# A two-layer streaming encoder on one core: the set-up gets its squares from a token-major copy of the input

## The chip, the cores and the metric

The kernel runs on one core of a Trainium2 chip. The metric is the device time of one execution in microseconds (us). Three runs of the kernel before took 1355.7, 1358.24 and 1358.74 us; the median is 1358.24 us.

The engines are named as in the profile: PE (TensorE, matrix multiplies; PEld is its weight loading), DVE (VectorE), ACT (ScalarE), POOL (GpSimd), SP (SyncE, whose queue issues the DMAs here). Each engine takes its own instructions in the order in which they stand in its queue: an instruction that waits holds everything behind it.

## The reference

512 tokens of width 1024 go through two layers, each a token mixer and a squared-ReLU MLP with residual additions, and a last RMSNorm. All is float32. What matters here is the beginning of the first mixer:

```python
y = _rmsnorm(h, norm_mix[0])            # h * rsqrt(mean(h*h) + eps) * w
proj = y @ w_in                         # 1024 -> 4112 columns
qkv  = silu(causal_conv(proj[..., :3072]))   # 8 heads of q, k, v
a, b = proj[..., 4096:4104], proj[..., 4104:]
beta = sigmoid(b)
g    = -exp(a_log) * softplus(a + dt_bias)   # log decay of each head
q, k = l2norm(q), l2norm(k)
o    = gated_delta_rule(q, k, v, beta, g)    # chunked, with a triangular solve per head
```

After it come the gate, the output projection, an MLP, the second layer (HGRN2 and an MLP), and the final norm.

## The kernel before

The input is kept with channels on the 128 partitions: eight tiles x[c] of 128 channels by 512 tokens. A product with a weight matrix is made exact enough by splitting both sides in two parts of a shorter float type: weights into `whi` and `wlo` (a cast by ACT, line 114, a subtraction by DVE or POOL, line 115), activations into `yh` and `yl` (lines 216 to 219). For each of the eight channel tiles k, a block of 128 output columns takes three matmuls: whi with yh, whi with yl, wlo with yh (lines 125 to 127). A block is thus 24 matmuls of 128x128 by 512 into one PSUM bank, called `pj`. Weights come in pairs of blocks: a raw tile of 128x8x256 (1 MB), split into whi and wlo.

The RMSNorm's factor (one number per token) is not needed for the products: they are made of x*w, and the factor, `rB`, multiplies the result when DVE takes it out of PSUM (line 389, tile `z`). So the sum of squares may come late.

`setup` loads x and the first two weight pairs in slices of 1, 1, 2, 2 and 2 channel tiles, so that the first four blocks can start early. For each x[c], ACT makes yh and squares x (lines 160, 163), DVE makes yl, and POOL or DVE adds the square to `sqacc` (line 165). For pair 0 POOL makes wlo, for pair 1 DVE. Two matmuls on a tile of zeros (line 240, `warm`) run before the first data is there.

`gdn` then asks for six blocks (four of the wide first group and two of the third pair), and after them issues, at high priority, `rstd_rows` and `gdn_decay`: `rstd_rows` splits sqacc, sums it over partitions with two matmuls into `ps` (line 195), and computes rB on rows of 512 (lines 197 to 206, ACT with Ln and Exp between). `gdn_decay` multiplies all of y by the 16 columns for a and b: 16 matmuls of 32 columns into `pab` (line 335); from pab*rB follow the cumulated log decays through `pt`, `pg` and `prow` (lines 337 to 378).

Then head by head: `gdn_conv` takes three blocks out of PSUM (line 389) and applies the four-tap convolution (a scale by ACT, line 391, three multiply-adds by DVE, line 393) into `kq` (k and q of a head side by side) and `v`; `gdn_silu` applies SiLU on ACT (line 85), with a table load before and after (line 91); `gdn_local` transposes k, q and v on PE (`pk` line 436, `pq` 443, `pv` 456), and makes the decay mask (`pe`, `e`, line 465) and the chunk products (`pga` line 475, `n`, `aa`). After every second head `gdn_inverse` solves two heads' triangular systems with many 32x32 matmuls (`px`, `pu`).

The order on each engine is not the program's order: the framework schedules the whole program before the run, by modelled times and priorities, and the result is fixed: whatever is late on the chip, each engine keeps the listed order. Tiles come from pools with a fixed number of buffers per name; a new tile waits until an old one of that name is free. In the trace SP issues a DMA, once eight are under way, when the one eight before it has landed.

Of the kernel before, what the change touches and what calls it, by code (L numbers as in the profile page):

```python
# [23 lines left out]
EPS = 1e-6  # L24
WARM = 384
# [8 lines left out]
class Net:  # L34
# [62 lines left out]
    def weight_tiles(self):  # L97
# [4 lines left out]
        return (tile("raw", F32, 2), *(tile(t + "3", F32R, 1) if last else tile(t, F32R, 2) for t in ("whi", "wlo")))  # L102
# [64 lines left out]
    def rstd(self):  # L167

        nc = self.nc
        ps = self.mix("ps")  # L170
        for c in range(NC):
            nc.tensor.matmul(ps[:, c:c + 1], lhsT=self.sq[:, c * P:(c + 1) * P], rhs=self.ones,
                             start=True, stop=True)
# [49 lines left out]
    def renew(self, c, norm, sq_eng="g", act=False):  # L223

        with self.tc.high_priority(offset=3000 if c == NB - 1 else 0):
            self.y[c] = self.split_norm(c, self.nw[:, norm * NB + c:norm * NB + c + 1], act)
            self.square_into(c == 0, self.h[c], sq_eng)


    def setup(self, w):  # L230

        nc = self.nc
# [3 lines left out]
        zeros = self.work("gate", bufs=2)  # L236
        nc.vector.memset(zeros, 0.0)
        warm = self.mix("warm", [P, WARM])
        for _ in range(2):
            nc.tensor.matmul(warm, lhsT=zeros[:, 0:P], rhs=zeros[:, 0:WARM], start=True, stop=True)  # L240
# [21 lines left out]
        return [(hi, lo) for _, hi, lo in pairs]  # L262
# [8 lines left out]
    def gdn(self, first):  # L271
        nc, a = self.nc, self.a
# [9 lines left out]
        abraw = self.work("gate", [P, NB, 2 * NH], bufs=2)  # L282
        nc.sync.dma_start(out=abraw, in_=a["gdn_ab"])
        ab = self.work("x", [P, NB, 4 * NH], F32R)
        hi = ab[:, :, 0:2 * NH]
        nc.scalar.copy(out=hi, in_=abraw)
        nc.vector.tensor_tensor(out=ab[:, :, 2 * NH:], in0=abraw, in1=hi.bitcast(F32), op=ALU.subtract)
# [41 lines left out]
    def gdn_decay(self, ab, alog, dtb):  # L329

        nc = self.nc
        pab = self.mix("pab", [4 * NH, T])
        for k in range(NB):
            for i, y in enumerate(self.y[k]):
                nc.tensor.matmul(pab, lhsT=ab[:, k], rhs=y, start=(k == 0 and i == 0), stop=(k == NB - 1 and i == 1))
# [656 lines left out]
def layout(x, gdn_w_in, gdn_conv, gdn_a_log, gdn_dt_bias, gdn_onorm, gdn_w_out, hgrn_w_in, hgrn_lb_logits,  # L992
           hgrn_gnorm, hgrn_w_out, norm_mix, norm_mlp, mlp_w_up, mlp_w_down, norm_final):
    i = np.arange(P)
    block = lambda start, h: np.arange(start + h * P, start + (h + 1) * P)
    o = {"x": x[0].T.reshape(NB, P, T).transpose(1, 0, 2)}
# [40 lines left out]
```

## Time and profile before

| | |
|---|---|
| median of three runs | 1358.24 us |
| the profiled execution | 1358.3 us, of which the span of instructions 1356.4 us |
| PE busy | 1330.5 us (98%) |
| DVE / ACT / POOL busy | 820.1 / 547.0 / 170.8 us |
| granted TensorE clock, mean of the span | 0.994 |

The span runs from the first instruction to the last; 1.9 us lie outside it. [...] A view of waits names the engine and the instruction that an engine last waited for; a view of windows gives the busy time of every engine in a stretch, and the granted clock.

### The profile page before, as it was taken

What the parts mean: (1) busy time and instruction counts of PE and PEld (TensorE: products, weight loads), DVE (VectorE), ACT (ScalarE), POOL (GpSimd) and SP (SyncE); (2) the same over time, 40 slices, a digit from 0 to 9 for tenths busy, and PEclk for the clock granted to TensorE, in tenths of its full rate; (3) what the DMA queues carried; (4) which work ended last, traced back from release to release, by engine and by line L of the source; (5) the groups of instructions that cost most, each with busy time, mean ns of one, the idle gap of its engine ahead of it and who ended that gap; (6) DMA issues with size and microseconds to landing.
All of it is one profiled execution on the core that took longest, in us unless ns stands there. A gap on an engine that the chain in (4) does not pass through costs nothing.

```text
span 1356.4 us, 24202 instructions
## 1 busy us (share of the span) xinstructions
PE 1330.5 (98%) x10340; PEld 1102.9 (81%) x10340; DVE 820.1 (60%) x1408; ACT 547.0 (40%) x1016; POOL 170.8 (13%) x172
## 2 busy tenths in 40 slices
PE   7999999999999999999999999999999999999997
PEld 5777777877888888888888898898888888888897
DVE  5896877765944444444473897787674444445453
ACT  5663556454344214233123555545344313214242
POOL 4001020200200120201220010000100020110222
PEclk8999999999999999999999999999999999999999
DMA  6131111221332222222231311121142223232242
GB/s 200 40 118 35 62 64 34 79 79 64 124 113 100 94 97 93 94 93 94 93 97 42 111 65 64 64 94 64 63 155 93 93 96 113 93 104 93 93 141 78
DMA packets 23356, 121.57 MB, mean 90 GB/s; under 512 B 3664, under 2 KB 6864, under 8 KB 9680
## 3 DMA queue, kind: packets, MB, share of 16 engines
q1 hardware_dynamic: 23248, 120.02, 26.3%
q8 instruction: 81, 1.33, 0.4%
q14 instruction: 27, 0.22, 0.0%
HBM read 117.91 MB, written 2.10 MB: 88 GB/s over the span
## 4 chain that ended last, share of the span: by engine, by line
PE 89%; DVE 5%; ACT 2%; issue 1%; DMA 1%; POOL 0%; SPq 0%; POOLq 0%; DVEq 0%; ACTq 0%
PE pj L126 25%; PE pj L127 25%; PE pj L125 25%; PE pj L714 1%; PE pj L715 1%; PE pj L713 1%; PE pga L475 1%; PE gr L786 1%; PE pu L520 1%; PE px L513 1%; DVE whi L742 1%; DVE wlo L115 1%; PE pw L590 1%; DVE kq L393 1%; DVE ol L742 1%
## 5 line engine op out<-in xcount | busy, mean ns | idle before, releaser
L114 ACT CAST whi<-raw 128x1024 fp32r<-128x1024 f32 (+2 forms) x222 | 220.9, 1024 | 410.0 <-PE pj L126 396.6
L125 PE MATMUL pj<-yh,whi 128*128 128x512 f32 x960 | 381.0, 397 | 0.9 <-ACT whi L114 0.9
L126 PE MATMUL pj<-yl,whi 128*128 128x512 f32 x960 | 381.3, 397 | 0.0
L115 DVE TENSOR_TENSOR wlo<-raw,whi 128x1024 fp32r<-128x1024 f32 (+2 forms) x217 | 289.7, 1348 | 151.0 <-ACT whi L114 148.7
L127 PE MATMUL pj<-yh,wlo 128*128 128x512 f32 x960 | 380.0, 396 | 0.0
L125 PEld LDWEIGHTS pj<-yh,whi 128*128 128x128 f32 x960 | 181.7, 189 | 37.6 <-ACT whi L114 2.0
L126 PEld LDWEIGHTS pj<-yl,whi 128*128 128x128 f32 x960 | 181.9, 189 | 36.0
L127 PEld LDWEIGHTS pj<-yh,wlo 128*128 128x128 f32 x960 | 181.2, 189 | 36.2 <-POOL wlo L115 0.3
L126 PE MATMUL pj<-ol,whi 128*128 128x512 f32 x336 | 131.3, 391 | 0.0
L898 DVE TENSOR_TENSOR gate<-pj,rB 128x512 f32<-128x512 f32 x56 | 38.6, 691 | 148.2 <-PE pj L127 148.2
L125 PE MATMUL pj<-oh,whi 128*128 128x512 f32 x320 | 125.1, 391 | 0.0
L127 PE MATMUL pj<-oh,wlo 128*128 128x512 f32 x320 | 125.0, 391 | 0.0
L884 ACT ACTIVATE z<-pj 128x512 f32<-128x512 f32 x64 | 38.0, 594 | 113.7 <-PE pj L127 109.6
L900 POOL TENSOR_TENSOR kd<-kd,gate 128x512 f32<-128x512 f32 x18 | 23.3, 1293 | 462.2 <-DVE gate L898 462.2
L126 PEld LDWEIGHTS pj<-ol,whi 128*128 128x128 f32 x336 | 63.2, 188 | 13.0
L125 PEld LDWEIGHTS pj<-oh,whi 128*128 128x128 f32 x320 | 60.1, 188 | 12.5 <-issue 0.3
L127 PEld LDWEIGHTS pj<-oh,wlo 128*128 128x128 f32 x320 | 60.0, 188 | 12.2
L165 POOL TENSOR_TENSOR sqacc<-sqacc,z 128x512 f32<-128x512 f32 x25 | 38.0, 1519 | 245.9 <-ACT z L163 241.8
L127 PE MATMUL pj<-kq,wlo 128*128 128x512 f32 (+1 forms) x192 | 67.8, 355 | 0.5 <-DVE wlo L115 0.5
L125 PE MATMUL pj<-kq,whi 128*128 128x512 f32 (+1 forms) x192 | 68.0, 354 | 0.0
L126 PE MATMUL pj<-kq,whi 128*128 128x512 f32 (+1 forms) x192 | 67.9, 354 | 0.0
L742 DVE TENSOR_TENSOR whi<-whi 128x256 f32<-128x256 f32 x112 | 49.9, 447 | 6.4 <-ACT whi L745 4.8
(379 smaller groups left out, 1941.0 us busy)
## 6 DMA issues: line engine op xcount, KB each, us to landing
raw<-down SPq DMA_DIRECT2D x36, 1024.0 KB, 4.9
raw<-up SPq DMA_DIRECT2D x32, 1024.0 KB, 4.8
raw<-gdn_in SPq DMA_DIRECT2D x14, 1024.0 KB, 4.8
raw<-hgrn_fq SPq DMA_DIRECT2D x8, 1024.0 KB, 4.9
raw<-gdn_out SPq DMA_DIRECT2D x4, 1024.0 KB, 5.4
raw<-hgrn_i SPq DMA_DIRECT2D x4, 1024.0 KB, 5.0
raw<-hgrn_gate SPq DMA_DIRECT2D x4, 1024.0 KB, 4.8
raw<-hgrn_out SPq DMA_DIRECT2D x4, 1024.0 KB, 4.9
```

The costliest lines, as they stand in the source:

```text
L114: self.nc.scalar.copy(out=hi[:, k], in_=raw[:, k])
L115: eng.tensor_tensor(out=lo[:, k], in0=raw[:, k], in1=hi[:, k].bitcast(F32), op=ALU.subtract)
L125: mm(o, lhsT=hi[:, k, c], rhs=yh, start=(k == 0), stop=False)
L126: mm(o, lhsT=hi[:, k, c], rhs=yl, start=False, stop=False)
L127: mm(o, lhsT=lo[:, k, c], rhs=yh, start=False, stop=(k == NB - 1))
L165: e.tensor_tensor(out=self.sq, in0=self.sq, in1=t, op=ALU.add)
L393: nc.vector.scalar_tensor_tensor(out=dst[:, s:], in0=z[:, :T - s], scalar=w[:, 3 - s:4 - s], in1=dst[:, s:], op0=ALU.mult, op1=ALU.add)
L475: mm(pga[:, c - c2], lhsT=ck(k, c), rhs=kq[:, :, c * P:(c + 1) * P], start=True, stop=True)
L742: mul = lambda o, x, y: nc.vector.tensor_tensor(out=o, in0=x, in1=y, op=ALU.mult)
L884: nc.scalar.activation(out=z, in_=out, func=AF.Relu)
L898: nc.vector.tensor_tensor(out=t, in0=out, in1=self.r2b, op=ALU.mult)
L900: e.tensor_tensor(out=self.h[c], in0=self.h[c], in1=t, op=ALU.add)
```

## The change

1. The squares no longer come from the channel-major x. A second copy of the input, `xt`, four tiles of 128 tokens by 1024 channels (512 KB each), is loaded during the set-up, and ACT squares each with a sum over its row: `sums[:, c]` has the sum of squares of 128 tokens. The eight squares of x[c], the additions into sqacc and `rstd_rows` go for this first norm; `rstd(self.sums)` takes the sums, works on 128x4 numbers, and spreads the result by four small matmuls into `pb`, from which ACT copies rB.
2. All wlo of the set-up are made by DVE; POOL makes none.
3. The weights for a and b are loaded and split early (after the second slice). The 16 products into `pab` are issued in the program after the first four blocks and before the blocks of the third pair.
4. The third pair is loaded in `setup` in four quarters into free `ol` tiles, and split there; it takes no raw buffer. `stream` takes it from `first`.
5. `warm` is nine matmuls of 128x128 by 128 in place of two of 128x128 by 384, on a smaller zero tile.

```diff
-WARM = 384
+WARM = 9
...
+        first = first or [self.weights(src[i]) for i in range(wide)]
         if wide:
-            first = first or [self.weights(src[i]) for i in range(wide)]
-            yield from self.project([(w, b) for w in first for b in (0, 1)], y, tokens)
+            yield from self.project([(w, b) for w in first[0:wide] for b in (0, 1)], y, tokens)
         for i in range(wide, n):
-            w = self.weights(src[i])
+            w = first[i] if i < len(first) else self.weights(src[i])
...
-    def rstd(self):
+    def rstd(self, sums=None):
...
+        if sums is None:
+            sums = self.mix("ps")
...
-        nc.vector.tensor_scalar(out=x, in0=ps[:, 0:NC], scalar1=1.0 / D, scalar2=EPS,
+        nc.vector.tensor_scalar(out=x, in0=sums[:, 0:NC], scalar1=1.0 / D, scalar2=EPS,
...
+        self.sums = self.cp.tile([P, NC], F32, tag="sums", name="sums")
         start = 0
-        for end in (1, 2, 4, 6, 8):
+        for end, chunks in ((1, ()), (2, ()), (4, (0,)), (6, (1, 2)), (8, (3,))):
...
-                self.renew(c, 0, "g" if c % 2 or c == 0 else "v", act=True)
+                self.y[c] = self.split_norm(c, self.nw[:, c:c + 1], act=True)
             for i, (raw, hi, lo) in enumerate(pairs):
                 nc.sync.dma_start(out=raw[:, k], in_=w[i][:, k])
-                self.split_weights(raw, hi, lo, k, (nc.gpsimd, nc.vector)[i])
+                self.split_weights(raw, hi, lo, k, nc.vector)
+            for c in chunks:
+                t = self.work("kq", [P, 2 * T], bufs=4)
+                nc.sync.dma_start(out=t, in_=self.a["xt"][:, c])
+                nc.scalar.activation(out=t, in_=t, func=AF.Square, accum_out=self.sums[:, c:c + 1])
+            if end == 2:
+                raw = self.work("gate", [P, NB, 2 * NH], bufs=2)
+                nc.sync.dma_start(out=raw, in_=self.a["gdn_ab"])
...
         self.ident = self.const("ident", [P, P])
+        third = self.weight_tiles(raw=False)
+        for i in range(0, NB, 2):
+            raw = self.work("ol", [P, 2, 256], bufs=NH)
+            nc.sync.dma_start(out=raw, in_=w[2][:, i:i + 2])
+            self.split_weights(raw, *(t[:, i:i + 2] for t in third), slice(0, 2), nc.vector)
...
-        blocks = chain([next(blocks) for _ in range(6)], blocks)
+        ready = [next(blocks) for _ in range(4)]
+        pab = self.mix("pab", [4 * NH, T])
...
+                nc.tensor.matmul(pab, lhsT=self.ab[:, k], rhs=y, start=(k == 0 and i == 0),
+                                 stop=(k == NB - 1 and i == 1))
+        ready += [next(blocks) for _ in (0, 1)]
+        blocks = chain(ready, blocks)
         with self.tc.high_priority(offset=3000):
-            self.rb = self.rstd_rows()
-            self.gdn_decay(ab, alog, dtb)
+            self.rb = self.rstd(self.sums)[1]
+            self.gdn_decay(pab, alog, dtb)
```

The schedule of the first mixer comes out another way on every engine; from the output projection on, the engines' orders are the same as before.

On PE, among the first four blocks (pj_223 to pj_226), at the fifth channel tile (yh_146), the kernel before has:

```order
L126 MATMUL pj_223<-yl_147,whi_84 128x512
L127 MATMUL pj_223<-yh_146,wlo_85 128x512
L195 MATMUL ps_385<-z_381,one 128x512
L125 MATMUL pj_224<-yh_146,whi_84 128x512
L126 MATMUL pj_224<-yl_147,whi_84 128x512
L195 MATMUL ps_385<-z_382,one 128x512
L127 MATMUL pj_224<-yh_146,wlo_85 128x512
```

The two matmuls into ps, which need the finished sum of squares, stand before the last 45 of the 96 matmuls of the four blocks; 16 of pab follow 19 matmuls later.

In the changed kernel the four blocks are pj_238 to pj_241, and the first matmuls that need the squares (pb) stand at their very end, with the rest of pab behind:

```order
L126 MATMUL pj_241<-yh_181,whi_93 128x512
L127 MATMUL pj_241<-yl_182,whi_93 128x512
L183 MATMUL pb_415<-ident,rsr_409 128x128 x4
L128 MATMUL pj_241<-yh_181,wlo_94 128x512
L309 MATMUL pab_338<-yl_102,x_125 32x512
L309 MATMUL pab_338<-yh_113,x_125 32x512
```

So pab, which stood after 70 of the 96 matmuls of these blocks, now stands after all of them (but for one of its 16), and the squares are wanted 44 block matmuls later.

On PE before the transposes of the second head (pk_705, of kq_490), the kernel before has, after the last block of the third pair (pj_356):

```order
L127 MATMUL pj_632<-yh_131,wlo_595 128x512
L125 MATMUL pj_632<-yh_146,whi_594 128x512
L126 MATMUL pj_632<-yl_147,whi_594 128x512
L125 MATMUL pj_671<-yh_93,whi_664 128x512
L126 MATMUL pj_671<-yl_94,whi_664 128x512
L436 MATMUL pk_705<-ident,kq_490 128x128 x4
L443 MATMUL pq_718<-ident,kq_490 128x128 x4
L127 MATMUL pj_601<-yh_146,wlo_595 128x512
```

Between the end of pj_356 and pk_705 it has 30 matmuls of the next three blocks (14 of pj_601, 14 of pj_632, 2 of pj_671).

The changed kernel has at the same place, from the third matmul after the end of pj_380 (its last block of the third pair) to the transposes of the second head (pk_713, of kq_498):

```order
L126 MATMUL pj_640<-yh_101,whi_601 128x512
L473 MATMUL pv_561<-ident,v_475 128x128 x4
L479 MATMUL pe_570<-sqacc_467,both 128x512
L127 MATMUL pj_640<-yl_102,whi_601 128x512
L126 MATMUL pj_679<-yh_101,whi_671 128x512
L127 MATMUL pj_679<-yl_102,whi_671 128x512
L492 MATMUL pga_581<-kq_474 128x256 x2
L492 MATMUL pga_587<-kq_474 128x256 x2
L453 MATMUL pk_713<-ident,kq_498 128x128 x4
L460 MATMUL pq_726<-ident,kq_498 128x128 x4
L128 MATMUL pj_609<-yh_101,wlo_602 128x512
```

Six matmuls of the next three blocks stand there in place of 30; the other 24 have moved behind the second head's transposes.

On DVE the changed kernel has, up to the last multiply-add of kq_498:

```order
L494 SCALAR_TENSOR_TENSOR n_579<-pga_587,nd_546,e_521 128x128 x2
L496 TENSOR_TENSOR aa_580<-pga_587,e_521 128x256
L523 STREAM_TRANSPOSE xd_971<-n_579 32x128 x4
L410 SCALAR_TENSOR_TENSOR kq_498<-z_506,conv,kq_498 128x509
L410 SCALAR_TENSOR_TENSOR v_499<-z_512,conv,v_499 128x511
L116 TENSOR_TENSOR wlo_602<-raw_603,whi_601 128x1024
```

The work of the first head and the second head's convolution come in the same sequence as before, but the two splits of weights by DVE that stood among them (the third pair's second half and the fourth pair's first half) stand earlier and later.

## Rows read from the trace of the kernel before

**Rows 1.** The page: busy time of each engine, and the granted clock in 40 slices of 34 us.

```profile
PE 1330.5 (98%) x10340; PEld 1102.9 (81%) x10340; DVE 820.1 (60%) x1408; ACT 547.0 (40%) x1016; POOL 170.8 (13%) x172
...
PEclk8999999999999999999999999999999999999999
```

**Rows 2.** PE's waits from 0 to 130 us: what waited and for what, us in total, times, longest.

```profile
PE ps L195 <- ACT one L257: 5.3, 1, 5.3
PE pu L520 <- issue: 2.1, 1, 2.1
...
PE pk L436 <- ACT kq L85: 0.4, 1, 0.4
PE pv L456 <- ACT v L85: 0.4, 1, 0.4
PE px L553 <- DVE wlo L548: 0.3, 1, 0.3
```

**Rows 3.** The chain that ended last, from 17 to 26 us: start, length, what.

```profile
18.13 0.68 DVE wlo L115
18.81 1.20 DVE yl L219
...
20.41 0.74 DVE yl L219
21.15 0.61 DVE sqacc L165
...
21.90 1.66 POOL sqacc L165
...
23.59 0.62 ACT z L191
24.35 0.80 PE ps L195
```

**Rows 4.** Windows around that wait: stretch, length, busy us (and instructions) of PE, PEld, DVE, ACT, POOL, granted clock, DMA share, GB/s.

```profile
18.99:24.35 5.36, 0.02 (x2) 0.00 (x1) 3.56 (x6) 1.68 (x4) 3.40 (x3) 0.82 0.07 14
24.35:29.20 4.85, 4.85 (x11) 3.79 (x12) 2.30 (x3) 1.54 (x4) 1.52 (x3) 0.50 0.69 240
29.20:35.40 6.20, 6.20 (x28) 3.82 (x27) 2.69 (x5) 2.00 (x2) 0.00 (x0) 0.99 0.40 155
```

**Rows 5.** The timeline of ACT and PE in the first 13 us, in four places: start, length, engine, line, what. The rows are the first block matmuls, the first cast for the third channel tile, and the first and a later matmul at a shorter length.

```profile
5.25 1.22 PE L125 MATMUL pj<-yh,whi 128*128 128x512 f32 x2 [0.88 <-ACT whi L114]
...
8.82 0.40 PE L126 MATMUL pj<-yl,whi 128*128 128x512 f32 x1
...
10.95 0.60 ACT L114 CAST whi<-raw 128x512 fp32r<-128x512 f32 x1
...
12.51 0.39 PE L125 MATMUL pj<-yh,whi 128*128 128x512 f32 x1
```

**Rows 6.** The timeline of SP's queue: the issue of DMA 20, 24 and 27 (each when DMA 12, 16 and 19, of 256 KB, has landed).

```profile
12.37 0.33 SPq L58 DMA_DIRECT2D ident<-ident  x1
...
15.08 0.33 SPq L58 DMA_DIRECT2D ident<-ident  x1
...
17.08 0.33 SPq L58 DMA_DIRECT2D onorm<-onorm  x1
```

**Rows 7.** The chain that ended last, near 722 us: the four spreading matmuls of a later norm in the same form as the new ones.

```profile
722.50 0.97 PE pb L180 x8
```

**Rows 8.** PE's timeline at half and at full clock, and up to the transposes of the second head.

```profile
26.65 0.63 PE L125 MATMUL pj<-yh,whi 128*128 128x512 f32 x1
...
27.07 0.63 PE L126 MATMUL pj<-yl,whi 128*128 128x512 f32 x1
...
64.05 0.39 PE L125 MATMUL pj<-yh,whi 128*128 128x512 f32 x1
64.27 0.39 PE L126 MATMUL pj<-yl,whi 128*128 128x512 f32 x1
...
64.96 0.60 PE L436 MATMUL pk<-ident,kq 128*128 128x128 f32 x4
```

**Rows 9.** One window, from the start of DVE's pab*rB to the end of the second head's last multiply-add into kq; then DVE's group of weight splits in that window (count, busy us, mean ns of one).

```profile
35.44:63.68 28.24, 28.15 (x136) 22.71 (x135) 25.38 (x68) 19.36 (x46) 1.61 (x2) 1.00 0.11 38
...
L115 DVE TENSOR_TENSOR wlo<-raw,whi 128x1024 fp32r<-128x1024 f32 x2 | 2.4, 1209 | 0.0
```

**Rows 10.** ACT's timeline: the SiLU of the second head's kq, with its wait.

```profile
63.78 1.06 ACT L85 ACTIVATE kq<-kq 128x1024 f32<-128x1024 f32 x1 [2.08 <-DVE kq L393]
```

**Rows 11.** Windows in the first solve of triangular systems, columns as in rows 4.

```profile
101.00:103.00 2.00, 0.51 (x41) 0.42 (x42) 1.19 (x2) 0.00 (x0) 0.00 (x0) 1.00 0.07 25
103.00:105.00 2.00, 1.38 (x26) 1.12 (x26) 0.93 (x2) 0.00 (x0) 0.35 (x1) 0.85 0.00 0
105.00:107.00 2.00, 2.00 (x11) 1.14 (x11) 0.51 (x2) 1.06 (x1) 1.75 (x7) 0.50 0.03 8
107.00:109.00 2.00, 2.00 (x38) 1.49 (x36) 0.00 (x0) 0.73 (x2) 1.75 (x5) 0.80 0.00 0
```

**Rows 12.** The timelines of DVE and POOL at 15 us: a subtraction of DVE beside one of POOL, and one alone.

```profile
15.91 1.75 POOL L115 TENSOR_TENSOR wlo<-raw,whi 128x512 fp32r<-128x512 f32 x1
16.42 1.78 DVE L165 TENSOR_TENSOR sqacc<-sqacc,z 128x512 f32<-128x512 f32 x1
18.13 0.68 DVE L115 TENSOR_TENSOR wlo<-raw,whi 128x512 fp32r<-128x512 f32 x1
```

More of the change, by code (lines that the diff above doesn't have):

```diff
@@ L94, in table, with weight_tiles @@
         self.last_switch, self.since_switch = i, []
-    def weight_tiles(self):
+    def weight_tiles(self, raw=True):
         tile = lambda tag, dt, bufs: self.wp.tile([P, NB, 256], dt, tag=tag, bufs=bufs, name=self.name(tag))
@@ L101, in weight_tiles @@
         last = self.nw_tiles % 3 == 0 and not self.two
-        return (tile("raw", F32, 2), *(tile(t + "3", F32R, 1) if last else tile(t, F32R, 2) for t in ("whi", "wlo")))
+        split = [tile(t + "3", F32R, 1) if last else tile(t, F32R, 2) for t in ("whi", "wlo")]
+        return [tile("raw", F32, 2)] + split if raw else split
     def weights(self, src):
@@ L165, in square_into @@
             e.tensor_tensor(out=self.sq, in0=self.sq, in1=t, op=ALU.add)
-    def rstd(self):
+    def rstd(self, sums=None):
         nc = self.nc
[L170 to L173, printed above, removed]
+        if sums is None:
+            sums = self.mix("ps")
+            for c in range(NC):
+                nc.tensor.matmul(sums[:, c:c + 1], lhsT=self.sq[:, c * P:(c + 1) * P], rhs=self.ones,
+                                 start=True, stop=True)
         x = self.work("rsx", [P, NC])
-        nc.vector.tensor_scalar(out=x, in0=ps[:, 0:NC], scalar1=1.0 / D, scalar2=EPS,
+        nc.vector.tensor_scalar(out=x, in0=sums[:, 0:NC], scalar1=1.0 / D, scalar2=EPS,
                                 op0=ALU.mult, op1=ALU.add)
@@ L234, in setup @@
         self.h, self.y = [], [None] * NB
-        zeros = self.work("gate", bufs=2)
+        zeros = self.work("e", [P, P])
         nc.vector.memset(zeros, 0.0)
-        warm = self.mix("warm", [P, WARM])
-        for _ in range(2):
-            nc.tensor.matmul(warm, lhsT=zeros[:, 0:P], rhs=zeros[:, 0:WARM], start=True, stop=True)
+        warm = self.mix("warm", [P, P])
+        for _ in range(WARM):
+            nc.tensor.matmul(warm, lhsT=zeros, rhs=zeros, start=True, stop=True)
         pairs = [self.weight_tiles() for _ in (0, 1)]
+        self.sums = self.cp.tile([P, NC], F32, tag="sums", name="sums")
         start = 0
-        for end in (1, 2, 4, 6, 8):
+        for end, chunks in ((1, ()), (2, ()), (4, (0,)), (6, (1, 2)), (8, (3,))):
             k = slice(start, end)
@@ L248, in setup @@
                     self.nw = self.const("norms", [P, 5 * NB])
-                self.renew(c, 0, "g" if c % 2 or c == 0 else "v", act=True)
+                self.y[c] = self.split_norm(c, self.nw[:, c:c + 1], act=True)
             for i, (raw, hi, lo) in enumerate(pairs):
                 nc.sync.dma_start(out=raw[:, k], in_=w[i][:, k])
-                self.split_weights(raw, hi, lo, k, (nc.gpsimd, nc.vector)[i])
+                self.split_weights(raw, hi, lo, k, nc.vector)
[6 more added lines that the diff above has]
+                nc.sync.dma_start(out=raw, in_=self.a["gdn_ab"])
+                self.ab = self.work("x", [P, NB, 4 * NH], F32R)
+                hi = self.ab[:, :, 0:2 * NH]
+                nc.scalar.copy(out=hi, in_=raw)
+                nc.vector.tensor_tensor(out=self.ab[:, :, 2 * NH:], in0=raw, in1=hi.bitcast(F32), op=ALU.subtract)
             start = end
         self.ident = self.const("ident", [P, P])
+        third = self.weight_tiles(raw=False)
[3 more added lines that the diff above has]
+            self.split_weights(raw, *(t[:, i:i + 2] for t in third), slice(0, 2), nc.vector)
         self.ones = self.const("ones", [P, 1])
@@ L261, in setup @@
         self.ident32 = self.const("ident32", [P, B])
-        return [(hi, lo) for _, hi, lo in pairs]
+        return [(hi, lo) for _, hi, lo in pairs] + [third]
     def load_x(self, c):
@@ L280, in gdn @@
         nc.sync.dma_start(out=dtb, in_=a["dtb"].partition_broadcast(P))
[L282 to L287, printed above, removed]
-        blocks = self.stream(a["gdn_in"][0:3 * NH // 2], self.y, first, 2, spare=1)
-        blocks = chain([next(blocks) for _ in range(6)], blocks)
+        blocks = self.stream(a["gdn_in"][0:3 * NH // 2], self.y, first, 2, spare=1)
+        ready = [next(blocks) for _ in range(4)]
+        pab = self.mix("pab", [4 * NH, T])
+        for k in range(NB):
+            for i, y in enumerate(self.y[k]):
+                nc.tensor.matmul(pab, lhsT=self.ab[:, k], rhs=y, start=(k == 0 and i == 0),
+                                 stop=(k == NB - 1 and i == 1))
+        ready += [next(blocks) for _ in (0, 1)]
+        blocks = chain(ready, blocks)
         with self.tc.high_priority(offset=3000):
-            self.rb = self.rstd_rows()
-            self.gdn_decay(ab, alog, dtb)
+            self.rb = self.rstd(self.sums)[1]
+            self.gdn_decay(pab, alog, dtb)
         self.two = True
@@ L327, in slot, with gdn_decay @@
         return self.extra[tag] if h % n == n - 1 else self.work(tag, shape, bufs=n - 1)
-    def gdn_decay(self, ab, alog, dtb):
+    def gdn_decay(self, pab, alog, dtb):
         nc = self.nc
[L332 to L335, printed above, removed]
         zab = self.work("z", [4 * NH, T], bufs=3)
```

6 lines of the change are left out of this document (3 added, 3 removed).

## The prediction

> **What bounds the kernel now.** I read the page first, for the engine that is full and for the slices where it is not. PE is busy for 1330.5 of 1356.4 us, and the granted clock is below 1.0 in the first slice of 34 us only [rows 1]. Then PE's waits, to see what it lacks: up to 130 us there is one large wait, 5.3 us before line 195, and four small ones [rows 2]. Then the chain of waits around the large one: it runs through DVE and POOL (yl, the additions into sqacc) to ACT and only then to PE [rows 3]. PE had block matmuls with their data there, but the two matmuls into ps stand ahead of them. Last the windows: in 5.36 us PE does nothing, and when it goes on it has 4.85 us at clock 0.50 before it is back at 1.0 [rows 4]. So the set-up is bound by PE's place in its own queue and then by the clock. Behind it, PE and DVE are both full: from 35.44 to 63.68 us, 28.15 and 25.38 of 28.24 us [rows 9]. That second row is what decides this change.
>
> **The set-up, term by term.** The sums go by the profiled execution (1358.3 us, span 1356.4 and 1.9 outside), which lies at the median of 1358.24.
>
> The stop before ps goes: +5.34. In the changed order nothing among the four blocks wants the squares before pb, which stands 44 block matmuls later.
>
> The slow clock behind it goes: half of 4.85 us [rows 4], +2.4.
>
> Two matmuls into ps go: at full clock one costs 0.228 us from start to start [rows 8] (64.05, 64.27), +0.5. Four small matmuls into pb come: 0.97 us as eight passes [rows 7], -1.0.
>
> The start: before, the first block matmul begins at 5.25, the first at the short length at 8.82, and the third channel tile at 12.51, though the cast of its weights began at 10.95 [rows 5]. With a warm-up that runs into the first data, I expect the clock up by about 6 us (after the stop it took 4.85 us of work [rows 4], and the warm-up starts a little after 1 us). The third tile's weights then bound: their cast ends at 11.55, or a little earlier without the square before it and 0.2 later for the 64 KB of a/b weights put ahead (a quarter of 0.67, below). I take 11.5, +1.0; without the clock it is 0.
>
> Set-up: 5.3 + 2.4 + 0.5 - 1.0 + 1.0 = 8.2 us. What hides the additions: xt brings 2 MB, three of its tiles and 64 KB ahead of the last weight slice. DMAs of 256 KB land 0.67 us apart (7 of them from 12.37 to 17.08 [rows 6]), so the slice lands 6.25 x 0.67 = 4.2 us later, at 21.3 instead of 17.1. PE wants it at 11.5 + 48 x 0.228 + one pab = 22.7: hidden by 1.4. The last xt lands 1.3 later, its squares take about 1.3 on ACT (1024 wide, as the SiLU of [rows 10], and the sum's read), then come casts, Ln, Exp and small DVE steps with two weight splits between, some 2.5: pb can start near 26.3, and PE gets there at 28. Hidden by 1.7. The wlo that POOL made go to DVE at 0.68 each where DVE is alone, and DVE loses the three stretches to 1.78 us beside POOL [rows 12]: DVE keeps up.
>
> **Behind the set-up: a new stop.** pab ended before at 35.44, with 26 block matmuls (5.9 us) still to do; now at 35.4 + 5.9 - 8.2 = 33.1, with none. From there both engines have a fixed list up to the transposes of the second head.
>
> DVE: 25.38 us of work [rows 9] less the two weight splits that are no longer between, 2.4, so 23.0. Its waits were 28.24 - 25.38 = 2.9 in all; they may go or stay. I take 1.2, since the one for PE's small decay products stays and the one for a finished block goes. Then SiLU and its hand-over, from 63.68 to 64.96 [rows 8, 9, 10]: 1.3. The transposes can start 25.5 us after pab (24.3 to 27.2), at 58.6.
>
> PE: 64.96 - 35.44 = 29.5 us, all full [rows 9], less the block matmuls that are not there now. Before there were 26 + 24 + 24 + 30 = 104, now 24 + 24 + 6 = 54: 50 x 0.228 = 11.4 less, 18.1 left.
>
> So PE stands for 25.5 - 18.1 = 7.4 us (6.2 to 9.1) before pk of the second head, and what is behind pk in its queue, the 24 moved block matmuls first of all, stands too, though its weights' casts are there. DVE and ACT are not held: they are what PE waits for. A check from the other side: pk comes 64.96 - 58.6 = 6.4 us earlier, with 24 matmuls (5.5 us) more still to do, so 0.9 is left of 8.2.
>
> After such a stop the clock falls: it did after 5.36 us without work, for 4.85 us at 0.50 [rows 4]. I charge the same, -2.4; the lower end is 0, if the small products before it count.
>
> The first instructions after this stop are transposes, and no row has transposes right after one. [...]
>
> **Further on.** Before, PE loses 0.4, 0.4 and 0.3 us to ACT and DVE later on, 2.1 to no visible releaser [rows 2], and after that a low clock: 2 x 0.15 + 2 x 0.50 + 2 x 0.20 = 1.7 us of full-speed work [rows 11]. In the changed kernel DVE runs some 6 us earlier there while PE is about where it was, so the 1.1 of waits should go; of the 3.8 I take half, 1.9, since that stretch is scheduled anew and may stall again or not. From the second layer on nothing changes its order.
>
> Sum: 8.2 - 7.4 - 2.4 + 1.1 + 1.9 = 1.4 us less, and some tenths either way: **1356.8 us**. The bounds: set-up 8.2, stop 6.2, no slow clock, all 4.9 further on give 7 us less, 1351.4. Stop 9.1, slow clock and nothing further on give 3.3 more, 1361.6.
>
> **Rivals.**
> *The whole gain stays.* The place is the same pk: if DVE were there as early as PE, the end would come 8.2 us earlier, 1350. For it: PE's only large wait before was the one that goes [rows 2], and DVE has little to do in the last microseconds of the set-up. Against: DVE cannot start on the blocks before pab*rB, which waits for pab, and its list from there has hardly a gap [rows 9]. 0.15.
>
> *A second stop makes it slower.* The place is the first triangular solve, a run of 32x32 matmuls in which each level waits for a DVE or ACT step of the one before. Before, it held one stop of 2.1 us and a low clock of 1.7 [rows 2, 11]. The new order reaches the solve with fewer block matmuls done and others between its levels; if it has that stop twice, the sum is 8.2 - 7.4 - 2.4 - 3.8 = 5.4 more, 1363.7. It decides the sign when what is lost there passes 1.3 us more than before beside a slow clock after the new stop. For it: small matmuls have too little work to cover a DVE step. Against: DVE has slack there now. 0.15.
>
> *The DMA is late.* If xt and the weights land a third slower than [rows 6], the last slice comes some 4 us later (17 pieces of 256 KB at 0.22 more), PE stops about 2.4 there, and pab and all behind it shift as much: 1359.2. For it: all of 7 MB now go through one queue in one go. Against: the pace in [rows 6] was already that of full queues. This is also the case in which the change does not do what it says, as the squares would come as late as before. 0.1.
>
> The forecast has the rest, 0.6.
>
> **How the numbers follow.** What a measurement of this kernel can tell from no change is about 0.2%, 2.7 us: faster is below 1355.5, slower above 1361. Of the forecast's 0.6, spread over 1351.4 to 1361.6 about 1356.8, I put 0.21 below, 0.35 within and 0.04 above. The first rival adds 0.15 to faster, the second 0.13 to slower and 0.02 within, the third 0.08 within and 0.02 above. Faster 0.36, same 0.45, slower 0.19. The forecast's own range is 1351.4 to 1361.6; the range given, 1349.5 to 1361.5, reaches down to the first rival's 1350 and leaves out the second (0.15) and a rest of the first: 2 in 10.
>
> **What would show it.** In the changed kernel's profile: no PE wait in the set-up, and pab ending near 33 us (the set-up's terms). A PE wait of 6 to 9 us before pk (its line is now 453), ended by ACT's SiLU near 58.6, with windows at clock 0.5 behind it (the stop and its price). PE's waits between 80 and 115 us smaller than 3.2 in sum (further on). I am wrong if that wait is under 3 us, since then most of 8.2 us must appear in the time; or if PE waits before pb or the last weight slice; or if losses in the solves or later in the mixer, which I only halved, are larger than all of this.

## The result: 0.24% slower, and the profile after

The changed kernel takes 1359.95 us in the median of 20 runs (1358.11 to 1363.94), the kernel before 1356.49 beside it (20 runs, 1355.44 to 1359.67). The ratio is 1.0024, 95% interval 1.0018 to 1.0031. I had forecast 1356.8, a little faster; that sum started from 1358.24, the median of three runs, 1.75 us above the median of the twenty here. The profiled execution after takes 1360.56 us with a span of 1358.8; before it was 1358.3 and 1356.4.

The page of the changed kernel, the rows that answer to [rows 1]: PE is busy as long as before, DVE and POOL less. The low clock has moved from the first slice of 34 us to the second, and so has the lowest busy share of PE in the first slices.

```profile
PE 1330.1 (98%) x10360; PEld 1104.7 (81%) x10360; DVE 815.4 (60%) x1411; ACT 546.9 (40%) x1018; POOL 155.2 (11%) x163
...
PE   9799999999999999999999999999999999999997
...
PEclk9799999999999999999999999999999999999999
```

PE's waits from 0 to 130 us in the changed kernel, which answer to [rows 2] (what waited for what, us in total, times, longest). The stop before ps is gone. Three waits at pk and pga have come, and at L530 one without a visible releaser.

```profile
PE pk L453 <- ACT kq L85: 4.4, 2, 4.1
PE pga L492 <- ACT x L85: 2.3, 1, 2.3
PE px L530 <- issue: 1.7, 1, 1.7
PE pga L492 <- DVE aa L496: 1.2, 1, 1.2
...
PE pj L126 <- ACT whi L115: 0.9, 1, 0.9
```

Where they lie, in PE's timeline of the changed kernel (start, length, what, in brackets the idle time before and what ended it):

```profile
6.33 0.39 PE L126 MATMUL pj<-yh,whi 128*128 128x512 f32 x1
...
51.34 1.27 PE L492 MATMUL pga<-kq 128*128 128x256 f32 x4 [2.35 <-ACT x L85]
53.80 2.05 PE L492 MATMUL pga<-kq 128*128 128x256 f32 x4 [1.19 <-DVE aa L496]
59.95 1.12 PE L453 MATMUL pk<-ident,kq 128*128 128x128 f32 x4 [4.10 <-ACT kq L85]
```

Between 49 and 60 us PE stands for 2.35 + 1.19 + 4.10 = 7.64 us. The clock over the same stretch, in windows with the columns of [rows 4]:

```profile
50.00:52.00 2.00, 0.66 (x3) 0.61 (x4) 2.00 (x7) 1.98 (x5) 0.00 (x0) 1.00 0.00 0
52.00:54.00 2.00, 0.81 (x4) 0.29 (x3) 1.51 (x5) 1.99 (x5) 0.00 (x0) 0.55 0.00 0
54.00:64.00 10.00, 5.90 (x18) 4.52 (x19) 9.03 (x20) 4.43 (x20) 1.26 (x1) 0.50 0.10 14
64.00:66.00 2.00, 2.00 (x7) 1.58 (x6) 2.00 (x5) 1.81 (x2) 0.00 (x0) 0.54 0.85 352
66.00:68.00 2.00, 2.00 (x13) 1.66 (x12) 1.53 (x8) 0.51 (x3) 0.00 (x0) 1.00 0.77 168
```

A window at 0.55 between the levels 1.00 and 0.50 tells where the step lies: the clock is low from 52.2 to 65.8 us. At 0.50 the block matmuls start 0.43 us apart (62.15, 62.58, 63.00), at 1.00 behind it 0.22 (65.93, 66.15). Of these 13.6 us PE works 8.35 and stands 5.3, so 4.2 us of full-speed work are lost. In the middle window DVE works 9.03 of 10 us: it is what PE waits for.

DVE's own list shows the other side. Two places in the changed kernel's timeline of DVE: the end of its wait for pab, and the low half of the fourth weight pair, without which PE has no more blocks to fill its wait.

```profile
33.03 0.68 DVE L354 TENSOR_TENSOR z<-pab,rB 32x512 f32<-32x512 f32 x1 [5.13 <-PE pab L309]
...
59.33 1.22 DVE L116 TENSOR_TENSOR wlo<-raw,whi 128x1024 fp32r<-128x1024 f32 x1
```

DVE sits idle for 5.13 us before pab ends, and then splits the weights that PE lacks only at 59.33, behind the second head's steps. These rows suggested the experiments.

### The profile page after: what moved, and what is told of

Its sections match the earlier page's. It is cut to its first block, busy times and chain, and to the rows that moved or that the text cites. A ratio compares the mean times of both kernels' runs of the same rounds, so it can differ in the third digit from the quotient of the medians.

```text
span 1358.8 us, 24234 instructions
## 1 busy us (share of the span) xinstructions
PE 1330.1 (98%) x10360; PEld 1104.7 (81%) x10360; DVE 815.4 (60%) x1411; ACT 546.9 (40%) x1018; POOL 155.2 (11%) x163
## 4 chain that ended last, share of the span: by engine, by line
PE 88%; DVE 6%; ACT 3%; issue 2%; DMA 0%; SPq 0%; POOL 0%; POOLq 0%; DVEq 0%; ACTq 0%
PE pj L128 25%; PE pj L127 25%; PE pj L126 25%; PE pj L732 1%; PE pj L731 1%; PE pj L730 1%; PE pga L492 1%; PE gr L803 1%; DVE wlo L116 1%; PE pw L607 1%; DVE whi L759 1%; PE px L530 1%; PE pu L537 1%; ACT L91 1%; ACT whi L115 1%
## 5 line engine op out<-in xcount | busy, mean ns | idle before, releaser
L115 ACT CAST whi<-raw 128x1024 fp32r<-128x1024 f32 (+2 forms) x220 | 219.2, 1024 | 402.5 <-PE pj L127 390.1
L166 POOL TENSOR_TENSOR sqacc<-sqacc,z 128x512 f32<-128x512 f32 x21 | 31.6, 1503 | 243.5 <-ACT z L164 243.4
```

Of the source, the lines that this page charges most:

```text
L115: self.nc.scalar.copy(out=hi[:, k], in_=raw[:, k])
L166: e.tensor_tensor(out=self.sq, in0=self.sq, in1=t, op=ALU.add)
```

## Experiments

Three theories. **A**: hurrying pab has brought forward DVE's list but not the blocks that PE runs beside it; the new stop and its slow clock give the set-up's gain back. **B**, a rival: DVE is the limit up to the first solve whatever PE does, so a stop that is taken away comes back later. **C**: part of the loss is waits without a releaser ("issue" in the profile), which depend on where instructions stand in PE's stream. Each ratio is to the kernel before, on the same chip.

**Both kernels again.** No edit.

> The changed kernel once more, to see what recurs. All theories: ratio to before 1.0018 to 1.0031, as in the first comparison, and PE's three waits on ACT and DVE between 48 and 60 us again (2.35, 1.19 and 4.10 us, sum 7.6) with the clock at 0.5 behind them. Theory A (the stop before the second head's pk eats the set-up's gain): nothing else of over 1 us is new. Theory C (the rest of the loss is PE waits without a visible releaser, set by where instructions stand in PE's stream): the 1.5 us wait at L732 near 900 us and the 1.7 us wait at L530 near 88 us come back within 0.5 us of these sizes at the same instructions. If those two waits are chance, they are gone or elsewhere.

> The kernel before against itself: ratio 0.9993 to 1.0007, the width of the measure. Theory C: its waits without a releaser at L520 (3.4 us in three, longest 2.1 us) come back at the same instructions. If they are chance: under 1.5 us in sum or at other instructions.

Measured: the changed kernel 1360.62 us, ratio 1.0025 (1.0016 to 1.0033); the kernel before against itself 0.9999 (0.9990 to 1.0007). The three waits at pga and pk came back to the tenth (2.3, 1.2, 4.1). The waits without a releaser came back at the same instructions, with other sizes: in the changed kernel L530 1.5 (1.7 the first time), L732 0.9 (1.5), L537 0.7 (1.0); in the kernel before L520 2.5 in two (3.4 in three), the longest 2.1 both times. So they belong to the program, and their sizes partly to the execution: the one at L520 that is missing in the second execution had 1.05 us in the first. Theory C had asked for L732 within 0.5 us; 1.46 and 0.93 are 0.53 apart, just outside that.

**The decay products behind six blocks again.**

```diff
-        ready = [next(blocks) for _ in range(4)]
+        ready = [next(blocks) for _ in range(6)]
         pab = self.mix("pab", [4 * NH, T])
...
-        ready += [next(blocks) for _ in (0, 1)]
```

> The changed kernel with the decay products behind six blocks again, as in the kernel before; the set-up stays new. The scheduler then lets DVE split two more weight pairs (four halves of 1.2 us) before the decay chain, so PE has blocks to run while DVE works on the second head. Theory A: PE waits less than 2 us in sum between 30 and 70 us (7.6 in the changed kernel), the clock stays at 1.00 there, and the set-up's 8 us are kept: ratio to before 0.993 to 0.997. Rival B (DVE is the limit up to the first solve whatever PE does, so the gain is lost to a later wait): the waits move behind 70 us and the ratio is 0.999 to 1.003.

Measured: 1360.61 us, ratio 1.0027 (1.0016 to 1.0037), as slow as the changed kernel. PE's timeline of this kernel, the rows with a wait of over 1 us between 60 and 90 us:

```profile
69.11 0.66 PE L452 MATMUL pk<-ident,kq 128*128 128x128 f32 x4 [2.12 <-ACT kq L85]
...
79.92 1.99 PE L491 MATMUL pga<-kq 128*128 128x256 f32 x8 [1.05 <-ACT v L474]
...
85.30 0.44 PE L529 MATMUL px<-wd,n 32*32 32x32 f32 x28 [3.38 <-DVE wd L523]
```

The stops are smaller and later, the largest in the first solve. In this order pab ends 11 us later than in the changed kernel (z after it starts at 44.04), because the third pair's blocks now really stand ahead of it. PE has work beside DVE, but all of DVE's list is late, and the solve pays. Theory A's forecast of 0.993 to 0.997 failed; rival B holds for this kernel.

**The fourth weight pair split early.** Everything as in the changed kernel, but the fourth pair is loaded and split with the decay chain's priority:

```diff
-            w = first[i] if i < len(first) else self.weights(src[i])
+            with self.tc.high_priority(offset=3000 if n == 12 and i == 3 else 0):
+                w = first[i] if i < len(first) else self.weights(src[i])
```

> The changed kernel, decay products behind four blocks, but the fourth weight pair loaded and split with the priority of the decay chain, into DVE's idle 5.1 us before pab ends. Theory A: the two low halves (2.4 us of DVE) free some 42 block matmuls, 9.6 us of PE work, for the 7.6 us of stops: PE waits under 2.5 us in sum between 30 and 70 us, clock near 1.00, ratio to before 0.993 to 0.997. Rival B: the same waits later, ratio 0.999 to 1.003. A third way: z after pab waits for the two splits (DVE takes them in order, and the weights land near 30 us), the decay chain comes 2 to 3 us late, ratio 0.996 to 1.000.

Measured: 1348.99 us, ratio 0.9951 (0.9937 to 0.9965), 11.6 below the changed kernel on the same chip. DVE's timeline in this kernel: the splits stand in the idle stretch, and z after pab starts 0.6 us later than in the changed kernel.

```profile
30.36 2.51 DVE L116 TENSOR_TENSOR wlo<-raw,whi 128x1024 fp32r<-128x1024 f32 x2 [5.31 <-DMA emask<-emask]
...
33.60 0.67 DVE L355 TENSOR_TENSOR z<-pab,rB 32x512 f32<-32x512 f32 x1
```

PE's windows in four stretches (columns as above), first of the changed kernel, then of this one:

```profile
0.00:30.00 30.00, 28.02 (x127) 22.82 (x128) 14.37 (x29) 19.34 (x37) 3.85 (x9) 1.00 0.81 269
30.00:70.00 40.00, 32.36 (x142) 24.71 (x141) 32.38 (x86) 26.34 (x73) 1.57 (x2) 0.83 0.26 91
70.00:130.00 60.00, 57.57 (x848) 45.25 (x847) 44.12 (x101) 28.79 (x64) 6.34 (x14) 1.00 0.17 60
130.00:400.00 270.00, 266.85 (x3017) 212.63 (x3016) 190.45 (x439) 132.41 (x343) 29.26 (x46) 1.00 0.23 75
```

```profile
0.00:30.00 30.00, 28.76 (x127) 23.71 (x128) 12.62 (x26) 18.03 (x33) 2.50 (x7) 1.00 0.88 294
30.00:70.00 40.00, 40.00 (x195) 31.94 (x194) 37.90 (x93) 29.63 (x79) 4.20 (x4) 1.00 0.28 88
70.00:130.00 60.00, 59.49 (x863) 46.52 (x861) 49.01 (x116) 32.37 (x87) 7.28 (x14) 1.00 0.19 67
130.00:400.00 270.00, 264.85 (x2999) 211.22 (x2999) 183.93 (x427) 129.53 (x325) 30.98 (x46) 1.00 0.23 76
```

From 30 to 70 us PE is busy for 40.00 us at clock 1.00, against 32.36 at 0.83. Every engine runs as many instructions as in the changed kernel: 2.5 us of DVE have moved by 29 us, and three of the four quarters of the third pair, split at 25 to 28 us in the changed kernel, now come behind them, two of these behind z. The gain of 11.6 is about what the stop and its slow clock took there, 7.6 + 4.2 us. That shows theory A for the changed kernel. With the run before it also shows the condition: PE must have blocks, and the chain behind pab must be early. Neither of the two kernels that have only one of these beats the kernel before.

**The fourth pair's low halves on POOL**, at the usual place:

```diff
-            self.split_weights(raw, hi, lo, slice(4 * i, 4 * i + 4), nc.vector)
+            self.split_weights(raw, hi, lo, slice(4 * i, 4 * i + 4), eng or nc.vector)
```

> The changed kernel with the fourth pair's low halves made by POOL instead of DVE, at the usual priority. Theory A: PE has the fourth pair's blocks before the second head's pk, so the stops of 7.6 us shrink to under 3 us; but DVE's steps beside POOL take longer (1.78 against 0.68 us alone), so DVE's work up to that pk is 1 to 4 us later than in the changed kernel: ratio to before 0.995 to 0.999. Rival B: the filler does not help, 1.000 to 1.003.

Measured: 1354.77 us, ratio 0.9987 (0.9978 to 0.9996). The wait at the second head's pk falls to 0.2 us, but PE waits 2.6 at prow in the decay chain. The timelines of POOL and of DVE show why: a step of 0.74 us takes 2.88 beside POOL.

```profile
38.43 5.37 POOL L116 TENSOR_TENSOR wlo<-raw,whi 128x1024 fp32r<-128x1024 f32 x2 [9.84 <-ACT whi L115]
```

```profile
37.97 0.74 DVE L410 SCALAR_TENSOR_TENSOR kq<-z,conv,kq 128x511 f32<-128x511 f32 x1
...
38.73 2.88 DVE L410 SCALAR_TENSOR_TENSOR kq<-z,conv,kq 128x509 f32<-128x509 f32 x1
```

**Parts of the change undone, on top of the early split.** The third pair through a full raw tile:

```diff
-        third = self.weight_tiles(raw=False)
...
-        return [(hi, lo) for _, hi, lo in pairs] + [third]
+        return [(hi, lo) for _, hi, lo in pairs]
```

> The early split with the third weight pair loaded the old way: a full raw tile, after the first pair's raw tile is free (about 24 us), instead of four quarters in free tiles. Theory A (the third pair in free tiles is what feeds PE from 33 us on): its two splits on DVE now come behind pab, near 34 to 38 us, PE waits 1 to 4 us at the first block of the third pair and the fourth pair's split goes back into DVE's busy stretch; ratio to before 0.996 to 1.000 against 0.995 with it. Rival E (it is not needed: the wide projection and pab keep PE fed until the pair is there): ratio 0.994 to 0.996, waits of PE between 30 and 70 us under 0.5 us.

The squares from the channel-major x:

```diff
+                self.square_into(c == 0, self.h[c], "g" if c % 2 or c == 0 else "v")
...
-                nc.sync.dma_start(out=t, in_=self.a["xt"][:, c])
-                nc.scalar.activation(out=t, in_=t, func=AF.Square, accum_out=self.sums[:, c:c + 1])
...
-            self.rb = self.rstd(self.sums)[1]
+            self.rb = self.rstd()[1]
```

> The early split with the squares undone: no token-major copy, eight squares of x on ACT, four additions on POOL and three on DVE, four small matmuls for the sums on PE, as in the kernel before but with the reciprocal root on small tiles. The prediction's first term (a stop of 5.3 us and 2.4 us of slow clock came from PE standing at the sums): if the sums are late again, PE waits 2 to 5 us at L176 or L184 between 20 and 30 us, the clock falls behind it, and the ratio is 0.997 to 1.001. If the small tiles alone were the cure: no wait, 0.995.

The old warm-up:

```diff
-        zeros = self.work("e", [P, P])
+        zeros = self.work("gate", bufs=2)
...
-        for _ in range(WARM):
-            nc.tensor.matmul(warm, lhsT=zeros, rhs=zeros, start=True, stop=True)
+        for _ in range(2):
+            nc.tensor.matmul(warm, lhsT=zeros[:, 0:P], rhs=zeros[:, 0:WARM], start=True, stop=True)
```

> The early split with the old warm-up (two matmuls of 384 columns on a 512-column tile instead of nine of 128 on a small one); nothing else differs on any engine. The prediction's term for the start: the blocks reach their short length 1.0 us later or more, PE's wait for the second group of weights (0.2 to 1.1 us near 11 us) takes part of it up, so 0.5 to 1.5 us slower than the early split, ratio 0.9955 to 0.9965. Rival: the weights bound the start anyway, no difference (0.995).

Measured: third pair 1356.48 us, 0.9999 (0.9991 to 1.0008); squares 1355.85 us, 0.9988 (0.9979 to 0.9997); warm-up 1348.48 us, 0.9934 (0.9921 to 0.9946). So with PE fed, taking back either of the first two parts costs some 7 us: the whole gain of the early split goes, or nearly. Without the third pair in free tiles PE waits between 30 and 70 us only 0.84 us at pt and 0.99 at a block, at the low end of what I expected, but the chain is late again: the first pk comes at 51.5 us against 47.2 with it. With the old squares PE stands 1.7 us at ps, below my 2 to 5, and the first pk is at 52.0. But the sums are not what it waits for: the last addition into sqacc ends at 22.7 us, and the row names the DMA of the constant `ones`, which this kernel issues at 23.74. So the 7 us are the price of this kernel's order with its late constant; what the late squares alone would cost is not shown. PE's timeline there:

```profile
28.80 1.02 PE L176 MATMUL ps<-ones,sqacc 128*128 128x1 f32 x8 [1.73 <-DMA ones<-ones]
```

The longer warm-up bought nothing that can be told: in both profiles the blocks are at their short length from 7.23 us on, and PE then waits for the third tile's weights, 0.86 us with the old one and 0.18 with the new. With the old one z behind pab starts at 34.12 us; the kernels with the new one and the same set-up (the early split and the four of the next experiment) spread from 33.60 to 34.30. My expectation of 0.5 to 1.5 us slower for the whole was wrong.

**Shifting PE's stream.** 16, 32 or 48 extra matmuls of 32x32 into unused columns of the sums' tile before the second layer; every engine's order stays the same:

```diff
+            for _ in range(16):
+                nc.tensor.matmul(sums[0:B, B:2 * B], lhsT=self.ident[0:B, 0:B], rhs=self.ident[0:B, 0:B],
+                                 start=True, stop=True)
```

> The kernel of the run before (fourth weight pair split early) with 16 extra 32x32 matmuls into unused columns behind the norm's sums before the second layer, near 709 us. No other engine's list and no other row of PE's list changes; every PE instruction behind them only stands later in PE's stream. Theory C (PE's waits without a releaser depend on where instructions stand in its stream): the 1.0 us wait at gr near 900 us changes by over 0.5 us or goes to another instruction, and the second layer's mixer (first gr to last, 164.8 us in the early split, 163.4 in the kernel before) takes 163.3 to 166. Rival D (such a wait belongs to the instruction itself or to transfers under way): it stays at the same gr within 0.3 us, and the mixer at 164.8 within 0.3. The extra matmuls themselves: under 0.5 us by 14 ns each (37 of them in 0.52 us).

> As the kernel with 16 extra matmuls, with 32. Theory C: another place or size of the waits without a releaser in the second layer's mixer than with 16 or with none. Rival D: the same wait as with none.

> As the kernel with 16 extra matmuls, with 48. Theory C: again another place or size; of the four shifts (0, 16, 32, 48) at least one has no wait without a releaser over 0.3 us in that mixer, which then takes 163.4. Rival D: the same wait as with none.

And a shift made by halving 16 block matmuls of the first MLP. It moves the stream half as far as the 16 extra matmuls, not as far, as I had expected: on the pages PE has 10360 matmuls without a shift, 10392 with 16 extra ones (two passes each) and 10376 with 16 halved, and as many weight loads.

```diff
+                cut = (0, n // 2, n) if self.cuts and k < NB - 1 else (0, n)
...
+                for p, q in zip(cut, cut[1:]):
+                    mm(o[:, p:q], lhsT=lo[:, k, c], rhs=yh[:, p:q], start=False, stop=(k == NB - 1))
```

> The early split with 16 of the block matmuls of the first MLP (near 330 us) cut into two halves of 256 columns: as many more PE instructions as the 16 extra small matmuls brought, so PE's stream behind them stands at the same offset as there, but without their 1 us (a half takes half the time). No list of another engine changes. Theory C: the second layer's mixer takes 163.4 to 163.7 us from first gr to last, as with that shift, without the 1.0 us wait at gr, and the time is 1 to 1.5 us below the early split's: ratio to before 0.993 to 0.9955. Rival D (the wait and its absence came by chance of an execution): 164.8 us and the wait at gr again.

Measured: 1350.82, 1352.91 and 1355.50 us for the three shifts (0.9954, 0.9971, 0.9991), 1349.45 (0.9942, 0.9930 to 0.9955) for the halves. The second layer's mixer, from the first matmul `gr<-ol` of 128x32 to the last, and its waits without a releaser in PE's list from 715 to 930 us:

| kernel | mixer, us | wait without releaser |
|---|---|---|
| before, twice | 163.4, 163.4 | none |
| changed, twice | 165.4, 164.7 | pj 1.5, 0.9 |
| early split | 164.8 | gr 1.0 |
| 16, 32, 48 extra | 163.5, 163.5, 164.0 | none, none, pj 0.3 |
| 16 halved | 164.0 | gr 0.2 |
| pab behind six blocks; splits on POOL; early split, old third pair | 164.9, 165.0, 164.8 | gr 0.9, 1.1, 0.9 |
| early split, old squares | 163.8 | gr 0.2 |
| early split, old warm-up | 163.5 | none |

PE's order in this stage is the same in all of them. Where the stream stands decides whether the wait is there: theory C is shown, rival D is out. The warm-up kernel is a shift too (fewer instructions at the start), and it also lost the 1.4 us wait at px at 163.5 us, in the second solve, that the early split has. For the halves, which move the stream only half as far, the mixer came to 164.0, not below 163.7, and their difference from the early split is inside the intervals. Here is one of these waits, in PE's timeline of the changed kernel, straight behind a run of 62 small matmuls:

```profile
898.47 0.71 PE L803 MATMUL gr<-ol 128*32 128x32 f32 x62
900.65 0.38 PE L732 MATMUL pj<-whi,yl 128*128 128x256 f32 x1 [1.46 <-issue]
```

What these waits have in common shows when they are set beside the arrival of PE's own instructions. Besides the queue of the loads the changed kernel's page has a DMA queue named "instruction" (packets, MB, share of the 16 DMA engines' span):

```profile
q8 instruction: 81, 1.33, 0.4%
```

These are 81 packets of 16 KB, while PE has 20801 instructions in the trace (matmuls, weight loads and a few waits), so one packet for each 256, by the count (20801 / 81 = 256.8). In the 14 profiles of this document PE has 30 waits without a releaser of 0.15 us or more behind 30 us. In 29 of them exactly 193 instructions more than a multiple of 256 have started before the wait ends (6 x 256 + 193 at 103.62 us in the kernel before, 61 x 256 + 193 at 900.65 in the changed one), whatever the instruction is; the thirtieth, 0.8 us at pt behind pab, is of another kind. Set side by side, packet n and the place n x 256 + 193: at all of some 1100 such places behind 30 us PE goes on no earlier than 1.2 us after the packet has landed, and at the 29 waits 1.2 to 1.6 us after. My reading of these places, not a view of its own: PE had run through a block of 256 instructions before it had the next one. In a run of small matmuls it gets through one in less time: the 62 before the wait at 900.65 take 0.71 us, and 62 block matmuls would take 14 by 0.228 each. A longer or shorter stream puts the end of a block at another instruction.

The shifts cost far more than the 0.5 us that I had set for the extra matmuls themselves. 16 of them are 32 passes and took 1.0 us, 48 took 3.1, in a row into the same columns; and with 16, 32 and 48 alike the clock was 0.83 over the ten microseconds from 710 us on, where the early split has 1.00. The two windows are of the kernel with 48, the second at a stop of 1.7 us in the first layer.

```profile
710.00:720.00 10.00, 10.00 (x128) 8.75 (x127) 1.38 (x6) 2.28 (x4) 0.00 (x0) 0.83 0.01 2
320.00:330.00 10.00, 8.20 (x31) 5.99 (x30) 6.13 (x18) 8.77 (x27) 0.00 (x0) 0.83 0.05 17
```

## Why the prediction was wrong, step by step

For the sums, PE's windows of the kernel before in the same four stretches, which have not been shown yet (columns as above). Idle time is length less PE's busy time, lost clock is what its clock lacks of 1.00 times the length.

```profile
0.00:30.00 30.00, 22.33 (x70) 16.24 (x71) 17.44 (x23) 17.85 (x34) 16.25 (x18) 0.89 0.63 206
30.00:70.00 40.00, 39.91 (x192) 31.13 (x191) 33.63 (x84) 25.07 (x67) 1.61 (x2) 1.00 0.20 69
70.00:130.00 60.00, 56.79 (x837) 43.86 (x836) 44.89 (x103) 30.56 (x68) 7.20 (x14) 0.97 0.22 72
130.00:400.00 270.00, 267.00 (x3018) 213.09 (x3017) 190.35 (x442) 133.52 (x349) 31.61 (x46) 1.00 0.23 76
```

**The set-up: right.** Before, z behind pab starts at 35.44 with 26 block matmuls (5.9 us) still to do, in the changed kernel at 33.03 with none: 8.3 us for the forecast 8.2, and 7.4 in the second pair of profiles (34.96 and 33.45). pb has no wait, the third tile starts at 11.51 (forecast 11.5). Whether the new warm-up is the reason for that last point is not shown: with the old one on top of the early split the third tile starts at 12.35 against 11.66, but the blocks are short as early. The +2.4 for the old stop's slow clock goes by one execution; in the second profile of the kernel before the low clock ends 3.6 us after that stop, not 4.85.

**The new stop: right in size and cause, half right in place.** 7.64 us for 7.4, and what PE waits for is DVE's list and ACT behind it; pk starts at 59.95 for 58.6. But only 4.10 us are the forecast wait for SiLU before pk. I had not seen that PE would be held already at pga, whose tile waits for Exp, so that nearly half of the stop comes there, from 49 us on.

**Its slow clock: too small.** I charged 2.4 us, the price of one stop with PE working straight on behind it. Here the stop came in three pieces, so the clock fell at 52.2 and the work between the pieces ran at half speed as well: 4.2. After the last piece the clock is back 5.9 us after pk starts, against 4.85 in [rows 4]. Whether transposes at the head of that stretch lengthen it these runs do not settle: in the second pair of profiles it is 4.7 against 3.6 us, and two executions of one kernel differ by as much as the two kernels do.

**Further on: the gain was too large.** I counted 3.0 us here: 1.1 for waits that go and 1.9 for half of a stop without a releaser and its clock. Idle time and lost clock from 30 us to 400 outside the new stop are about 8.0 us and 7.0 in the two profiles of the kernel before, and 5.6 and 6.9 in the two after, where a stop of 1.5 us at L530 once took the clock down as well. That is 1.2 us of gain, not 3.0. Between 70 and 130 us the waits for ACT and DVE, which were to go, fell from 1.1 to 0.7 us only. The stop without a releaser moved from L520 (2.1 us, at instruction 6 x 256 + 193) to L530 (1.7 and 1.5, at 4 x 256 + 193): the end of another block of 256 instructions now falls into the same solve; the slow clock behind it, 1.7 us, went in one of two executions, which is the half that I had counted. From 130 to 400 us PE stands 3.1 us instead of 2.5, as means of two.

**The second layer: left out.** I wrote that nothing changes its order, and nothing does. Yet its mixer takes 2.0 and 1.3 us longer, mostly in the wait at L732, where every instruction stands at another place in PE's stream and the end of a block of 256 (61 x 256 + 193) falls behind a run of 62 small matmuls.

Together, as means of the two pairs: -7.9 + 7.6 + 4.2 - 1.2 + 1.7 = 4.4 us slower, where the spans of the two pairs differ by 2.4 and 5.1, and the medians by 3.5.

**What failed, then,** is three terms of about the same weight: the slow clock, charged at 2.4 and measured at 4.2; the gain further on, counted at 3.0 and measured at 1.2; and the second layer, put at nothing and measured at 1.7 slower. Any one of them put right alone turns 1.4 us less into no more than 0.4 more, which these runs could not tell from nothing. In the first the mechanism was right and the size wrong. In the second the waits for ACT and DVE stayed, though DVE is earlier there. In the third the mechanism was wrong: I took an unchanged order for an unchanged time, but 29 of the 30 waits without a releaser stand at n x 256 + 193 in PE's instruction stream. That the time, 1359.95, lies within my 1349.5 to 1361.5 is luck: my sum started 1.75 us too high and was wrong in its sign.

Of the rivals, the second stop in the solve was the one that the order of pab behind six blocks turned into (3.38 us at px there); in the changed kernel itself it did not come. The first rival, the whole gain kept, is what the early split reaches: 8 us below the kernel before. My reason against it was right for the change as made, but what it named, DVE's list behind pab, could have told me the cure: the idle time ahead of that list.

## What to carry to other kernels

When a step that starts a long chain on one engine is hurried, look at what the waiting engine will run beside the chain, and whether its operands are made by the same engine behind the chain; if so, move them into the idle time before it (2.5 us of DVE moved here were worth 11.6 us). Price a stop in pieces by the whole stretch at low clock (4.2 us here), not by the idle time plus one recovery (2.4). And with PE's order in that stage unchanged, its place in the stream moved the second layer's mixer between 163.4 and 165.4 us here, so a gain of two or three microseconds in a program with such runs of small matmuls is judged over several orders or shifts, with the waits listed stage by stage.

## What the runs showed of the hardware that I had not expected

- The page counts 81 packets of 16 KB in the queue "instruction", one for each 256 of PE's 20801 instructions. In the 14 profiles 29 waits of PE of 0.2 to 2.1 us without a releaser stand at n x 256 + 193, last until 1.2 to 1.6 us after a packet has landed, and those in the second layer's mixer vanished, moved or shrank when the stream ahead was longer by 32 to 192 instructions. The same wait differed by 0.53 us between two executions (L732), and one of 1.05 us (L520) was missing in the other.
- After a stop of 1.7 us the clock was down in two kernels and not in two others. At the same instruction of the same order, near 325 us, the window of ten microseconds has a clock of 1.00 in the early split and with 16 extra matmuls, and 0.83 with 32 and 48, whose difference comes only some 385 us later: 1.7 us of chance in the time.
- 32x32 matmuls repeated into the same columns started 32 ns apart (32 passes in 1.0 us, with 16 extra matmuls); in the solve, where neighbours lie in different blocks of rows, the same shape started 9 ns apart (64 in 0.75 us at 99.33 in the kernel before, of which the last takes 0.19). My 14 ns of the expectation, 37 in 0.52 us, had counted the last one's length in.
